# A decoder layer on one core: an embedding gate ahead of the gated unit, the state space some steps later, 64-row taps, and a bias table from the host

## The chip, the cores and the metric

The kernel runs on one core of one Trainium2 chip. The metric is the device time of one execution in microseconds (us), the median of several runs. The engines are called as in the profile: PE is TensorE (matmuls), PEld its weight loads, DVE is VectorE, ACT is ScalarE, POOL is GpSimd, SP is SyncE, whose queue issues nearly all DMAs.

## What is computed

One layer of a hybrid decoder for 256 tokens of width 1024, all in float32. The input x is projected to eight parts; attention (8 heads of 64, one causal block with a bias by distance) and a state space (S5, 32 groups of 16 channels with 64 complex states each) run on some of them, gates on the others, and a normalisation ends it.

```python
proj = x @ w_in[i]
q, k, v, z_a, u, z_s, g_a, g_s = jnp.split(proj, IN_SPLITS, axis=-1)
o_a = moba_attention(heads(q), heads(k), heads(v), rel_bias)
y_a = (o_a * jax.nn.silu(z_a)) @ w_attn_proj[i]
y_s = s5_ssm(u, ssm_a_re[i], ssm_a_im[i], ssm_log_dt[i], ssm_b_re[i], ...)
glu_a, glu_b = jnp.split(jax.nn.gelu(y_s, approximate=False) @ w_glu[i], 2, axis=-1)
y_s = glu_a * jax.nn.sigmoid(glu_b)
y_s = (y_s * jax.nn.silu(z_s)) @ w_ssm_proj[i]
mix = (jax.nn.sigmoid(g_a) * y_a + jax.nn.sigmoid(g_s) * y_s) @ w_out[i]
ple = jax.nn.sigmoid(x @ w_ple_gate[i]) * (p[i] @ w_ple_proj[i])
x = layer_norm(DEEPNORM_ALPHA * x + mix + ple, ln_g[i], ln_b[i])
```

The "embedding gate" is sigmoid(x @ w_ple_gate), computed in two halves of 512 columns, tg0 and tg1. The "gated unit" (glu) needs the state space's output y; the embedding gate needs only x.

## The kernel before, in words

**Units and steps.** All weights are read once, in 62 units of 2 x 128 rows by 512 columns (512 KB). A unit is loaded by SP into one of 5 `raw` buffers, rounded by ACT into `whi` (3 buffers, L144), and the remainder is taken by DVE as `wlo` (3 buffers, L145). PE then multiplies in three terms (xh with whi, xl with whi, xh with wlo). One unit is one step of the main chain: 24 matmuls of 128 x 256 (`t_chunk`) or 12 of 128 x 512 (`n_chunk`). All matmuls are recorded at L149, the line of the helper `mm`, so they are told apart by their tiles: `acc` is the main chain, `aux` everything else. The steps in order of before: u 0 to 3, za 4 to 7, zs 8 to 11, q 12 to 15, k 16 to 19, v 20 to 23, ga 24 to 31, gs 32 to 39, ya 40 to 43, glu 44 to 47, tg0 48 to 51, tg1 52 to 55, and then the embedding projection, ys and w_out.

**Order.** PE executes in the order in which the code is written. On the other engines a scheduler orders the instructions, those of loads and splits with priority. `at(step, f)` says behind which step's matmuls the side work `f` is written; the table `AT` holds most of these numbers. A unit's `whi` takes the place of the one three steps earlier, so ACT can write it only when that step's matmuls have been read.

**Buffers of the side work.** Everything that PE makes beside the main chain goes to PSUM tiles `aux`, and there are four of these. Each is free again only when its last reader, mostly ACT or DVE, is through.

**The state space.** `s5_btT(part)` turns the matrices of B with 8 PE transposes, and ACT copies the two results to `BT` (L385). `s5_xm(part, half)` multiplies them with U in two `aux` tiles, 16 matmuls a block. (A matmul of plain float32 operands stands as two records in the profile, so this block is x32 there.) `s5_kbm(half)` makes the taps of the convolution inside a block of L = 4 tokens, 16 narrow matmuls (x32) into the tile `kp`. `s5_kbd` spreads these on DVE to full 128 x 128 block-diagonal weights `Kbd`; `s5_cabd` does that for the weights `CAb` with a POOL memset and ACT copies (L436). At the end `s5_yt(t)` (4 matmuls with `Kbd` for each t of 4, x8) and `s5_y(t)` (32 narrow matmuls with `CAb`, x64) add up one `aux` tile for each t.

**Attention.** `a_scores` puts two heads' scores in two `aux` tiles, DVE adds the bias from the table `tb` and takes the maximum, `a_exp` makes the exponentials on ACT (L587, behind one table load) and scales them (L592), `a_tr` and `a_out` transpose and multiply with v. The bias table is made by a matmul of `rel_bias` with a one-hot matrix in step 8, a copy, a store of 12 KB to DRAM and a load of 1 MB.

Of the kernel before, what the change touches and what calls it, by code (L numbers as in the profile page):

```python
# [18 lines left out]
P = 128  # L19
# [3 lines left out]
H = 8  # L23
# [6 lines left out]
NEG = -1.0e30  # L30
NWARM = 16

AT = dict(bt=24, x=27, sc=23, kb=27, cb=29, tr=31, out=32, y=35)

MAGIC = 12582912.0
LOG2E = 1.4426950408889634
# [6 lines left out]
TWO_PI = float(np.nextafter(np.float32(2 * math.pi), np.float32(0)))  # L43


C_ID, C_MK, C_J, C_OH = 0, P, P + 8, P + 8 + NPH
C_W = C_OH + 257
# [10 lines left out]
def hybrid_layer_kernel(ctx: ExitStack, tc, xT, x, pT, w_in, w_ap, w_sp, w_out, par, bp, cp,  # L58
# [19 lines left out]
    def aux():  # L78
        return PS("aux", 4)
# [9 lines left out]

    cs = T([P, C_W], "cst")  # L90
    ident = cs[:, C_ID:C_ID + P]
    mask = cs[:, C_MK:C_MK + 8]
    jmul = cs[:, C_J:C_J + NPH]
    onehot = cs[0:32, C_OH:C_OH + 257]

    NRAW, NHI, NLO = 5, 3, 3
    units = []
# [50 lines left out]
    def mm(o, a, b, start, stop):  # L148
        return PE.matmul(o, a, b, start=start, stop=stop, skip_group_check=True)  # L149
# [11 lines left out]
        add_units(w_in, D, COL["gs"] + 512 * n, 512)  # L161
    for n in range(2):
        add_units(w_ap, 512, 512 * n, 512)
    for n in range(2):
        add_units(w_glu, 512, 512 * n, 512)
    for n in range(2):
        add_units(w_pg, D, 512 * n, 512)
    for n in range(2):
        add_units(w_pp, 256, 512 * n, 512)
    for n in range(2):  # L170
# [32 lines left out]
    def par_loads():
        nc.sync.dma_start(cs, cst)
        nc.sync.dma_start(br, bp)
        nc.sync.dma_start(cr, cp)
    dk = T([P, 4], "dk")
    rb = T([32, 8], "rb")
    ptr = T([P, 2, S], "Ct")
    ph = T([P, 2, S], "ph", F32R)  # L210
    pl = T([P, 2, S], "pl", F32R)
# [206 lines left out]
                       st5[f"CA{part}"][:, gp, 0:4, :].rearrange("p n c -> p (n c)"),  # L418
                       part == 0, part == 1)

    def s5_kbd():
        p_ = st5["kp"]
        kb = st5["Kbd"] = T([P, 4, 4, P], "Kbd")
        V.tensor_tensor(out=kb.rearrange("p t u (g c) -> p (t u) g c", c=16),
                        in0=bc(p_[:, 0:256].rearrange("p (tu c) -> p tu c", c=16), 2, 8),
                        in1=bc(bc(mask, 1, 16), 3, 16), op=ALU.mult)
        for t in range(4):
            V.scalar_tensor_tensor(kb[:, t, 0, :], ident, dk[:, t:t + 1], kb[:, t, 0, :],
                                   op0=ALU.mult, op1=ALU.add)
# [83 lines left out]
    yh = []  # L513
    yl = []

    def s5_yt(t):
        p_ = st5[f"yp{t}"] = aux()
        kb = st5["Kbd"]
        for tau in range(4):
            n = (4 - tau) * NJ  # L520
            mm(p_[:, tau * NJ:4 * NJ], kb[:, t, tau, :],
               uT[:, t, 0:4 - tau, :].rearrange("p l j -> p (l j)"), tau == 0, False)

    def s5_y(t):
# [7 lines left out]
        if t == 0:  # L532
            st5["y"] = T([P, 4, S], "U")
# [12 lines left out]
    sm_ = T([P, H, 2], "sms")  # L546

    def a_bias():
        p_ = aux()
        nc.sync.dma_start(rb, relb)  # L550
        mm(p_[0:8, 0:257], rb, onehot, True, True)
        r8 = T([8, 384], "pt", bufs=2)
        V.memset(r8[:, 0:127], NEG)
        A.activation(r8[:, 127:384], p_[0:8, 0:257], AF.Copy)
        rs = dr.tile([8, 384], F32, name="scr_r")
        nc.sync.dma_start(rs, r8)
        nc.sync.dma_start(tb, bass.AP(tensor=rs.tensor, offset=rs.offset,
                                        ap=[[1, P], [384, H], [1, 256]]))

    def rev(h, last, n):  # L560
        a = tb[:, h, :]
# [193 lines left out]
    def ev_glu(n):  # L755
        def f(a):
            if n == 0:
                g = late["ga"] = T([P, 2, 512], "uT", nm="gluA")
                for s in range(2):
                    A.activation(g[:, s, :], a[s], AF.Copy, scale=0.25)  # L760
            else:
                g = late["gb"] = T([P, 2, 512], "U", nm="gluB")
                for s in range(2):
                    A.activation(g[:, s, :], a[s], AF.Tanh, scale=0.5)
                    V.scalar_tensor_tensor(g[:, s, :], g[:, s, :], 1.0, late["ga"][:, s, :],
                                           op0=ALU.add, op1=ALU.mult)
                    V.tensor_mul(g[:, s, :], g[:, s, :], zs[:, s, :])
                late["sh"] = T([P, 4, S], "Ct", F32R, nm="sh")
                late["sl"] = T([P, 4, S], "A1", F32R, nm="sl")
                for s in range(2):  # L770
                    h_ = late["sh"][:, 2 * s:2 * s + 2, :].rearrange("p k s -> p (k s)")
                    A.activation(h_, g[:, s, :], AF.Copy)
                    V.tensor_sub(late["sl"][:, 2 * s:2 * s + 2, :].rearrange("p k s -> p (k s)"),
                                 g[:, s, :], h_.bitcast(F32))
        return f
    for n in range(2):
        t_chunk(4, lambda: (yh[0], yl[0]), ev_glu(n))

    n_chunk(8, xop, ev_tanh(new("tg0", "CAb0", (P, 2, 512))))
    n_chunk(8, xop, ev_tanh(new("tg1", "CAb1", (P, 2, 512))))  # L780

    def ev_pp(n):
# [46 lines left out]
    def at(i, *f):  # L829
        order.setdefault(i, []).extend(f)  # L830
# [4 lines left out]
                f()  # L835
        return g

    at(0, par_loads)
    at(0, *[hp_(f) for f in (s5_scalars, s5_angles, s5_phases)])
    at(1, hp_(s5_abar))  # L840
    at(2, lambda: s5_bt(0), lambda: s5_bt(1))
    at(4, s5_bounce)
    at(8, a_bias)
    at(5, lambda: s5_ca(0), lambda: s5_ca(1))
    at(6, small_loads)
    at(AT["bt"], lambda: s5_btT(0))
    at(AT["bt"] + 1, lambda: s5_btT(1))
# [120 lines left out]
def _constants():  # L968
    c = np.zeros((P, C_W), np.float32)
    c[:, C_ID:C_ID + P] = np.eye(P, dtype=np.float32)  # L970
    c[:, C_MK:C_MK + 8] = (np.arange(P)[:, None] // 16 == np.arange(8)[None]).astype(np.float32)
    c[:, C_J:C_J + NPH] = np.concatenate([np.arange(5), L * np.arange(NJ)]).astype(np.float32)
    for d in range(257):
        b = d if d < 16 else min(31, 16 + int(math.log(d / 16) / math.log(8) * 16))
        c[b, C_OH + d] = 1.0
    return c


def _layout(i):
# [17 lines left out]


# [13 lines left out]
```

## Time and profile before

| what | value |
|---|---|
| time, median of 3 runs | 242.12 us (242.01 to 242.9) |
| the profiled execution | 242.09 us, its span 240.3 us |
| mean granted clock of TensorE in it | 0.995 of full speed |
| busy share of PE, DVE, ACT, POOL | 96%, 78%, 58%, 7% |
| data moved | 44.37 MB, mean 185 GB/s |

The span runs from the first to the last event of the core's engines; the time has 1.8 us more. A row of a timeline gives the start in the span, the busy time from the first instruction to the end of the last of the group, the operation, and in brackets the idle time before it and what released it. Groups overlap slightly, because the next matmul or activation begins before the last has drained.

### The profile page before, as it was taken

To read this page: it belongs to the slowest core of one execution; us is meant where nothing else is said; L and a number is where in the kernel's file an instruction comes from. 1 tells how busy PE (TensorE), PEld (TensorE's weight loads), DVE (VectorE), ACT (ScalarE), POOL (GpSimd) and SP (SyncE) were. 2 spreads that over 40 slices of the span, in tenths; PEclk is the share of its full clock that TensorE was granted. 3 is DMA by queue.
4 is the path that set the end of the run, shared out by engine and by line. 5 is a ranking of instruction groups with operands and counts; after the bars stand their busy time and mean duration, and the time that the engine had idled before them with its cause. 6 is when DMAs were issued, how large, how long until landed. Compare 5 with 4: busy or idle time off the path is not lost.

```text
span 240.3 us, 5066 instructions
## 1 busy us (share of the span) xinstructions
PE 230.3 (96%) x2042; PEld 212.6 (88%) x2042; DVE 188.2 (78%) x333; ACT 140.2 (58%) x222; POOL 15.9 (7%) x17
## 2 busy tenths in 40 slices
PE   8899999999999999999999999999999999999970
PEld 6899999999978899998998999999888889988760
DVE  2879999999899986878999744485674479997395
ACT  4847554845588389999734955335565353775021
POOL 4000000000000005000000000072000000000031
PEclk9999999999999999999999999999999999999998
DMA  5999998977634484323743663664555655660013
GB/s 162 331 343 357 354 238 242 353 232 215 196 93 118 147 255 119 110 92 97 232 150 136 207 213 110 197 245 162 189 174 191 199 202 170 186 190 0 3 44 131
DMA packets 26374, 44.37 MB, mean 185 GB/s; under 512 B 4200, under 2 KB 7280, under 8 KB 26352
## 3 DMA queue, kind: packets, MB, share of 16 engines
q1 hardware_dynamic: 26064, 43.75, 57.5%
q8 instruction: 16, 0.26, 0.4%
q10 hardware_dynamic: 288, 0.31, 0.4%
q14 instruction: 6, 0.05, 0.1%
HBM read 42.47 MB, written 1.59 MB: 183 GB/s over the span
## 4 chain that ended last, share of the span: by engine, by line
PE 77%; ACT 10%; DMA 5%; DVE 4%; SPq 2%; issue 1%; ACTq 0%
PE acc L149 68%; PE aux L149 8%; DMA raw<-in_w_in 5%; ACT whi L144 4%; ACT sc L587 2%; ACT sc L592 2%; ACT CAb L436 1%; DVE wlo L145 1%; SPq L191 1%; SPq L189 1%; DVE xb L930 1%; DVE xb L920 1%; DVE st L910 1%; DVE xb L908 1%; PE aux L598 0%
## 5 line engine op out<-in xcount | busy, mean ns | idle before, releaser
L144 ACT ACTIVATE whi<-raw 128x1024 fp32r<-128x1024 f32 (+2 forms) x71 | 70.7, 997 | 59.9 <-PE acc L149 52.9
L145 DVE TENSOR_TENSOR wlo<-raw,whi 128x1024 fp32r<-128x1024 f32 (+2 forms) x71 | 81.9, 1154 | 30.3 <-ACT whi L144 29.9
L149 PE MATMUL acc<-xh,whi 128*128 128x256 f32 x288 | 47.7, 287 | 0.8 <-ACT whi L144 0.8
L149 PE MATMUL acc<-xl,whi 128*128 128x256 f32 x288 | 45.8, 281 | 0.0
L149 PE MATMUL acc<-xh,wlo 128*128 128x256 f32 x288 | 45.6, 280 | 0.0
L149 PEld LDWEIGHTS acc<-xh,whi 128*128 128x128 f32 x288 | 39.3, 190 | 2.3 <-ACT whi L144 1.3
L149 PEld LDWEIGHTS acc<-xl,whi 128*128 128x128 f32 x288 | 39.3, 189 | 0.0
L149 PEld LDWEIGHTS acc<-xh,wlo 128*128 128x128 f32 x288 | 38.9, 188 | 0.3 <-DVE wlo L145 0.3
L149 PE MATMUL acc<-whi,xh 128*128 128x512 f32 x48 | 19.0, 395 | 0.0
L149 PE MATMUL acc<-wlo,xh 128*128 128x512 f32 x48 | 19.0, 395 | 0.0
L149 PE MATMUL acc<-whi,xl 128*128 128x512 f32 x48 | 19.0, 395 | 0.0
L149 PEld LDWEIGHTS acc<-wlo,xh 128*128 128x128 f32 x48 | 9.0, 188 | 2.2
L149 PEld LDWEIGHTS acc<-whi,xh 128*128 128x128 f32 x48 | 9.0, 188 | 2.1
L149 PEld LDWEIGHTS acc<-whi,xl 128*128 128x128 f32 x48 | 9.0, 188 | 2.1
L149 PE MATMUL acc<-whi,BT 128*128 128x512 f32 (+1 forms) x32 | 9.1, 366 | 0.0
L818 POOL TENSOR_SCALAR xb<-xb 128x1024 f32<-128x1024 f32 x2 | 5.5, 2774 | 42.2 <-DMA xb<-in_x 42.2
L916 ACT ACTIVATE rs<-mv,eps 128x1 f32<-128x1 f32 x2 | 0.6, 294 | 12.1 <-DVE mv L915 12.1
L587 ACT ACTIVATE sc<-sc,nmx 128x128 f32<-128x128 f32 (+1 forms) x16 | 7.0, 442 | 0.0
L149 PEld LDWEIGHTS acc<-whi,BT 128*128 128x128 f32 x32 | 5.7, 188 | 1.1
L193 DVE TENSOR_TENSOR xl<-sc,xh 128x256 fp32r<-128x256 f32 x8 | 3.4, 420 | 4.1 <-ACT xh L192 4.1
L908 DVE TENSOR_TENSOR xb<-acc,xb 128x512 f32<-128x512 f32 (+1 forms) x4 | 2.5, 619 | 5.0 <-PE acc L149 5.0
L928 POOL TENSOR_TENSOR xb<-xb,lng 128x512 f32<-128x512 f32 (+1 forms) x2 | 1.7, 839 | 69.8 <-ACT xb L927 69.8
(254 smaller groups left out, 407.8 us busy)
## 6 DMA issues: line engine op xcount, KB each, us to landing
raw<-in_w_in SPq DMA_DIRECT2D x36, 512.0 KB, 4.7
raw<-in_w_pg SPq DMA_DIRECT2D x8, 512.0 KB, 4.6
raw<-in_w_out SPq DMA_DIRECT2D x8, 512.0 KB, 4.5
raw<-in_w_ap SPq DMA_DIRECT2D x4, 512.0 KB, 5.0
raw<-in_w_glu SPq DMA_DIRECT2D x4, 512.0 KB, 3.9
raw<-in_w_sp SPq DMA_DIRECT2D x4, 512.0 KB, 4.1
raw<-in_w_in SPq DMA_DIRECT2D x7, 256.0 KB, 4.3
sc<-in_xT SPq DMA_DIRECT2D x8, 128.0 KB, 4.0
```

Source lines behind the costliest of these rows:

```text
L144: A.activation(h[:, k, c], r[:, k, c], AF.Copy)
L145: V.tensor_sub(l[:, k, c], r[:, k, c], h[:, k, c].bitcast(F32))
L149: return PE.matmul(o, a, b, start=start, stop=stop, skip_group_check=True)
L189: nc.sync.dma_start(xs[:, kk], xT[:, kk])
L191: nc.sync.dma_start(t[:, k, cc], units[c][:, k, cc])
L193: V.tensor_sub(xl[:, kk], xs[:, kk], xh[:, kk].bitcast(F32))
L436: A.activation(o[rw, :, :, 16 * g2:16 * g2 + 16], st5[f"CA{part}"][rw, :, 1:5, :], AF.Copy)
L587: A.activation(sc[:, h, qs[q]], sc[:, h, qs[q]], AF.Exp, bias=nmx[:, h, q:q + 1], accum_out=sm_[:, h, q:q + 1])
L592: A.activation(sc[:, h, qs[q]], sc[:, h, qs[q]], AF.Copy, scale=sm_[:, h, q:q + 1])
L818: G.tensor_scalar(late["xb"][:, s, :], late["xb"][:, s, :], ALPHA, None, op0=ALU.mult)
L908: V.tensor_tensor(out=xb[:, s, sl], in0=(yo2 if c0 else yo[s][n])[:, 0:c1 - c0], in1=xb[:, s, sl], op=ALU.add)
L910: V.bn_stats(out=stat[s][:, c // 256, :], in_=xb[:, s, c:c + 256])
```

## The change

The diff does four things. The first half of the embedding gate, with its four units, goes from behind the glu to ahead of it (tg0 44 to 47, glu 48 to 51). The table `AT` puts the state space's and the attention's later parts 2 or 3 steps further back. The weights of the taps are made another way: `s5_kt` writes them compactly with ACT copies, stores 512 KB to DRAM and loads it back in 8 DMAs into `tt`, and `s5_yt` multiplies in tiles of 64 rows and 32 columns, for two t at once, 64 matmuls (128 records) a call and two calls. The bias table comes from the host as 1 MB and is loaded by one DMA. Some small loads and `s5_abar` are written at another step, and the constants become smaller. In the rows of the kernel after, the line of `mm` is L147, the split is L142 and L143, the exponentials L594, their scaling L599, the copies to `BT` L378, and those of `CAb` L444.

```diff
-AT = dict(bt=24, x=27, sc=23, kb=27, cb=29, tr=31, out=32, y=35)
+AT = dict(bt=27, x=29, sc=23, kb=27, cb=29, tr=33, out=34, y=38)
...
+    add_units(w_pg, D, 0, 512)
     for n in range(2):
         add_units(w_glu, 512, 512 * n, 512)
-    for n in range(2):
-        add_units(w_pg, D, 512 * n, 512)
+    add_units(w_pg, D, 512, 512)
...
-    def s5_kbd():
-        p_ = st5["kp"]
-        kb = st5["Kbd"] = T([P, 4, 4, P], "Kbd")
-        V.tensor_tensor(out=kb.rearrange("p t u (g c) -> p (t u) g c", c=16),
-                        in0=bc(p_[:, 0:256].rearrange("p (tu c) -> p tu c", c=16), 2, 8),
-                        in1=bc(bc(mask, 1, 16), 3, 16), op=ALU.mult)
+    kscr = dr.tile([512, 4, 64], F32, name="scr_k")
+
+    def s5_kt():
+
+        p_ = st5["kp"][:, 0:256].rearrange("p (t u c) -> p t u c", t=4, u=4)
+        kt = T([P, 4, 4, 16, 4], "kT", nm="kt")
+        G.memset(kt, 0.0)
+        for l in range(L):
+            A.activation(kt[:, :, l, :, l:4].rearrange("p t c u -> p t u c"), p_[:, :, 0:4 - l, :],
+                         AF.Copy)
...
+        nc.sync.dma_start(kscr.rearrange("(t q) l d -> q t (l d)", q=P),
+                          kt.rearrange("q t l c u -> q t (l c u)"))
+        tt = st5["tt"] = T([P, 16, 2, 64], "Kbd", nm="tt")
+        G.memset(tt[:, :, 1, :], 0.0)
+        v = kscr.rearrange("(r m c) l d -> r l c m d", r=2, c=16)
+        for r in range(2):
+            for l in range(L):
+                b0 = 64 * r + 16 * (L - 1 - l)
+                nc.gpsimd.dma_start(tt[b0:b0 + 16, :, 0, :], v[r, l])
...
-    def s5_yt(t):
-        p_ = st5[f"yp{t}"] = aux()
-        kb = st5["Kbd"]
-        for tau in range(4):
-            n = (4 - tau) * NJ
-            mm(p_[:, tau * NJ:4 * NJ], kb[:, t, tau, :],
-               uT[:, t, 0:4 - tau, :].rearrange("p l j -> p (l j)"), tau == 0, False)
+    def s5_yt(t0):
+
+        for t in (t0, t0 + 2):
+            st5[f"yp{t}"] = aux()
+        tt = st5["tt"].rearrange("p m z d -> p (m z d)")
+        for l in range(L):
+            for g2 in range(2):
+                for gpt in range(4):
+                    for r in range(2):
+                        t = t0 + 2 * r
+                        gpp = 4 * (t % 2) + gpt
+                        rw = slice(64 * r, 64 * r + 64)
+                        o = 128 * (2 * gpp + g2) - 64 * g2 + l
+                        mm(st5[f"yp{t}"][32 * gpt:32 * gpt + 32, l * NJ:(l + 1) * NJ],
+                           tt[rw, o:o + 125:4], U[rw, gpp, g2, :], l == 0 and g2 == 0, False)
...
     def a_bias():
-        p_ = aux()
-        nc.sync.dma_start(rb, relb)
-        mm(p_[0:8, 0:257], rb, onehot, True, True)
...
-        nc.sync.dma_start(tb, bass.AP(tensor=rs.tensor, offset=rs.offset,
-                                        ap=[[1, P], [384, H], [1, 256]]))
+        nc.sync.dma_start(tb, relb)
...
+    n_chunk(8, xop, ev_tanh(new("tg0", "CAb0", (P, 2, 512))))
     for n in range(2):
         t_chunk(4, lambda: (yh[0], yl[0]), ev_glu(n))
-
-    n_chunk(8, xop, ev_tanh(new("tg0", "CAb0", (P, 2, 512))))
...
-    at(AT["kb"] + 1, lambda: s5_kbm(1), s5_kbd)
+    at(AT["kb"] + 1, lambda: s5_kbm(1), s5_kt)
...
-    for t in range(4):
-        at(AT["y"] + 2 * t, lambda t=t: s5_yt(t))
-        at(AT["y"] + 1 + 2 * t, lambda t=t: s5_y(t))
-    at(44, load_x)
+    for t in range(2):
+        at(AT["y"] + 4 * t, lambda t=t: s5_yt(t))
+        at(AT["y"] + 1 + 4 * t, lambda t=t: s5_y(t))
+        at(AT["y"] + 3 + 4 * t, lambda t=t: s5_y(t + 2))
+    at(47, load_x)
```

**ACT around the copies to BT.** Before, ACT's queue from the split for step 27 to the second head pair's exponentials reads so; the last four digits of a name count the tiles.

```order
69 L144 ACTIVATE whi_1150<-raw_1027 128x1024
70 L385 ACTIVATE BT_177_1111<-aux_1112 128x512
71 L385 ACTIVATE BT_177_1111<-aux_1118 128x512
72 L144 ACTIVATE whi_1217<-raw_1045 128x1024
73 L385 ACTIVATE BT_185_1178<-aux_1179 128x512
74 L385 ACTIVATE BT_185_1178<-aux_1185 128x512
75 L587 ACT_TABLE_LOAD
76 L587 ACTIVATE sc_158,sms_160<-sc_158,nmx_159 128x128
```

In the kernel after, the same queue has the table load first; here are its rows from the split of step 29's unit to the copies of the taps, with stretches left out.

```order
70 L142 ACTIVATE whi_1237<-raw_1069 128x1024
71 L594 ACT_TABLE_LOAD
...
83 L378 ACTIVATE BT_189_1265<-aux_1266 128x512
84 L378 ACTIVATE BT_189_1265<-aux_1272 128x512
85 L444 ACTIVATE CAb_209_1438<-C_97_504 64x64x16 x2
...
100 L142 ACTIVATE whi_1448<-raw_1235 128x1024
101 L594 ACTIVATE sc_158,sms_160<-sc_158,nmx_159 128x128
...
105 L594 ACTIVATE sc_158,sms_160<-sc_158,nmx_159 128x256
106 L378 ACTIVATE BT_199_1340<-aux_1341 128x512
107 L378 ACTIVATE BT_199_1340<-aux_1347 128x512
```

The copies of both parts now stand behind the table load, the second part's behind all 16 exponentials, four `CAb` copies, eight scaling copies and four splits.

**PE at the same place.** Before, the first product with U (tiles 1299 and 1300) stood two steps behind the second part's transposes (tiles 1179 and 1185, row 364). In the kernel after, PE has these rows around steps 28 and 29, numbered.

```order
419 L376 MATMUL aux_200_1341<-cst_2_82,A1_87_420 128x128 x4
420 L376 MATMUL aux_201_1347<-cst_2_82,A1_87_420 128x128 x4
421 L147 MATMUL aux_192_1288<-C0_97_504,Bbd_84_408 32x64 x4
...
425 L147 MATMUL acc_197_1314<-xh_3_84,whi_187_1237 128x256 x2
...
437 L147 MATMUL aux_207_1420<-U_27_155,BT0_189_1265 64x64 x2
438 L147 MATMUL aux_208_1421<-U_27_155,BT0_189_1265 64x64 x2
```

The product with U is now one step behind the second part's transposes. Its second tile, 1421, is given the buffer of tile 1341, which is free when ACT's row 106 has read it.

**POOL around the taps.** POOL's queue in the kernel after, from the memset of the compact taps on:

```order
8 L420 MEMSET kt_1369 128x1024
9 L441 MEMSET CAb_210_1442 128x2048
10 L432 MEMSET tt_1380 128x16x64
11 L441 MEMSET CAb_209_1438 128x2048
12 L476 MEMSET A_214_1492 128x16
13 L477 MEMSET A_215_1493 128x16
14 L437 DMA tt_1380<-scr_k 16x16x64 x8
15 L497 MEMSET B_231_1611 128x16
```

Eight DMAs stand in a queue that issued none before; they wait for the store of the taps to `scr_k`.

## Rows read from the trace of the kernel before

**Rows 1.** The page, part 1: busy time and instructions of PE.

```profile
PE 230.3 (96%) x2042; PEld 212.6 (88%) x2042; DVE 188.2 (78%) x333; ACT 140.2 (58%) x222; POOL 15.9 (7%) x17
```

**Rows 2.** Waits of the weight loads: waited for, us in total, times, longest.

```profile
PEld aux L149 <- ACT BT L385: 1.2, 2, 0.7
...
PEld aux L149 <- ACT pt L602: 0.4, 1, 0.4
```

**Rows 3.** Timeline of PE, steps 24 to 27: start, busy us, operation.

```profile
75.03 0.23 PE L149 MATMUL aux<-ks,qs 128*128 128x128 f32 x1
...
75.95 0.63 PE L149 MATMUL acc<-xh,whi 128*128 128x256 f32 x4
...
78.78 1.03 PE L383 MATMUL aux<-cst,A 128*128 128x128 f32 x8
...
84.17 1.03 PE L383 MATMUL aux<-cst,A 128*128 128x128 f32 x8
```

**Rows 4.** Timeline of PE, steps 28 and 29: blocks kbm and xm.

```profile
98.07 0.65 PE L149 MATMUL aux<-C,Bbd 128*32 128x64 f32 x32
...
101.67 0.69 PE L149 MATMUL aux<-U,BT 64*64 64x64 f32 x32
102.30 0.74 PE L149 MATMUL acc<-xh,whi 128*128 128x256 f32 x4
```

**Rows 5.** Timeline of ACT, 84 to 107 us.

```profile
84.86 1.06 ACT L385 ACTIVATE BT<-aux 128x512 f32<-128x512 f32 x2
85.94 1.28 ACT L587 ACT_TABLE_LOAD   x1
...
89.81 0.63 ACT L216 ACTIVATE ph<-Ct 128x512 fp32r<-128x512 f32 x1 [0.72 <-DMA Ct<-in_pT]
90.35 1.04 ACT L144 ACTIVATE whi<-raw 128x1024 fp32r<-128x1024 f32 x1
...
98.03 1.48 ACT L592 ACTIVATE sc<-sc,sms 128x128 f32<-128x128 f32 x4
...
102.62 4.25 ACT L436 ACTIVATE CAb<-C 64x1024 f32<-64x1024 f32 x4
106.89 1.09 ACT L726 ACTIVATE Bbd<-acc 128x512 f32<-128x512 f32 x2
```

**Rows 6.** The page, part 5: the exponentials.

```profile
L587 ACT ACTIVATE sc<-sc,nmx 128x128 f32<-128x128 f32 (+1 forms) x16 | 7.0, 442 | 0.0
```

**Rows 7.** Timeline of PE, one tap block and one block of y.

```profile
135.46 1.31 PE L149 MATMUL aux<-uT,Kbd 128*128 128x256 f32 x8
136.57 0.70 PE L149 MATMUL acc<-xh,whi 128*128 128x256 f32 x4
...
139.47 1.10 PE L149 MATMUL aux<-BT,CAb 128*32 128x64 f32 x64
```

**Rows 8.** Timeline of PE, the bias matmul.

```profile
31.55 0.63 PE L149 MATMUL acc<-xh,wlo 128*128 128x256 f32 x4
32.11 0.59 PE L149 MATMUL aux<-cst,rb 32*8 32x257 f32 x2
...
33.21 0.63 PE L149 MATMUL acc<-xl,whi 128*128 128x256 f32 x4
```

**Rows 9.** Windows: stretch, its us, busy us of each engine, PEclk, DMA share, GB/s.

```profile
233.00:236.00 3.00, 0.00 (x0) 0.00 (x0) 2.86 (x8) 0.76 (x2) 1.49 (x3) 1.00 0.25 94
...
237.00:240.00 3.00, 0.00 (x0) 0.00 (x0) 0.39 (x1) 0.00 (x0) 0.00 (x0) 0.65 0.48 170
```

**Rows 10.** Timeline of PE, the start.

```profile
0.76 3.57 PE L87 MATMUL aux<-const-bfloat16-1.0 128*128 128x256 bf16 x16 [0.76 <-PEq L1003]
4.10 1.27 PE L149 MATMUL acc<-xh,whi 128*128 128x256 f32 x4
```

**Rows 11.** DMA issues: KB each, median us to landing.

```profile
scr_u<-uT SPq DMA_DIRECT2D x1, 512.0 KB, 5.7
U<-scr_u SPq DMA_DIRECT2D x8, 64.0 KB, 6.6
```

More of the change, by code (lines that the diff above doesn't have):

```diff
@@ L43 @@
 TWO_PI = float(np.nextafter(np.float32(2 * math.pi), np.float32(0)))
-C_ID, C_MK, C_J, C_OH = 0, P, P + 8, P + 8 + NPH
-C_W = C_OH + 257
+C_J, C_M16, C_ID = 0, NPH, NPH + 16
+C_W = C_ID + P
 def bc(ap, axis, n):
@@ L91, in hybrid_layer_kernel @@
     ident = cs[:, C_ID:C_ID + P]
-    mask = cs[:, C_MK:C_MK + 8]
     jmul = cs[:, C_J:C_J + NPH]
-    onehot = cs[0:32, C_OH:C_OH + 257]
     NRAW, NHI, NLO = 5, 3, 3
@@ L201, in hybrid_layer_kernel @@
     cr = T([P, 2, GP, 16], "crw")
[L203 to L206, printed above, removed]
     dk = T([P, 4], "dk")
-    rb = T([32, 8], "rb")
     ptr = T([P, 2, S], "Ct")
@@ L419, in s5_kbm @@
                        part == 0, part == 1)
-    def s5_kbd():
-        p_ = st5["kp"]
-        kb = st5["Kbd"] = T([P, 4, 4, P], "Kbd")
-        V.tensor_tensor(out=kb.rearrange("p t u (g c) -> p (t u) g c", c=16),
-                        in0=bc(p_[:, 0:256].rearrange("p (tu c) -> p tu c", c=16), 2, 8),
-                        in1=bc(bc(mask, 1, 16), 3, 16), op=ALU.mult)
-        for t in range(4):
-            V.scalar_tensor_tensor(kb[:, t, 0, :], ident, dk[:, t:t + 1], kb[:, t, 0, :],
-                                   op0=ALU.mult, op1=ALU.add)
+    kscr = dr.tile([512, 4, 64], F32, name="scr_k")
[6 more added lines that the diff above has]
+                         AF.Copy)
+        m16 = bc(cs[:, C_M16:C_M16 + 16], 1, 4)
+        for t in range(4):
+            d = kt[:, t, 0, :, 0]
+            d = bass.AP(tensor=d.tensor, offset=d.offset, ap=[list(d.ap[0]), [65, 4], list(d.ap[1])])
+            V.scalar_tensor_tensor(d, m16, dk[:, t:t + 1], d, op0=ALU.mult, op1=ALU.add)
+        nc.sync.dma_start(kscr.rearrange("(t q) l d -> q t (l d)", q=P),
[7 more added lines that the diff above has]
+                nc.gpsimd.dma_start(tt[b0:b0 + 16, :, 0, :], v[r, l])
     def s5_cabd(part):
@@ L531, in s5_y @@
                        st5[f"CAb{part}"][:, gp, l, :], st5[hk][:, gp, :], False, l == 3 and part == 1)
-        if t == 0:
-            st5["y"] = T([P, 4, S], "U")
+        if "y" not in st5:
+            st5["y"] = T([P, 4, S], "uT", nm="y")
             yh.append(T([P, 4, S], "sn", F32R))
@@ L548, in a_bias @@
     def a_bias():
-        p_ = aux()
-        nc.sync.dma_start(rb, relb)
-        mm(p_[0:8, 0:257], rb, onehot, True, True)
[L552 to L556, printed above, removed]
-        nc.sync.dma_start(tb, bass.AP(tensor=rs.tensor, offset=rs.offset,
-                                        ap=[[1, P], [384, H], [1, 256]]))
+        nc.sync.dma_start(tb, relb)
     def rev(h, last, n):
@@ L836, in hp_ @@
         return g
-    at(0, par_loads)
+    at(0, lambda: nc.sync.dma_start(cs, cst))
     at(0, *[hp_(f) for f in (s5_scalars, s5_angles, s5_phases)])
-    at(1, hp_(s5_abar))
-    at(2, lambda: s5_bt(0), lambda: s5_bt(1))
+    at(3, lambda: nc.sync.dma_start(br, bp), hp_(s5_abar), lambda: s5_bt(0), lambda: s5_bt(1))
     at(4, s5_bounce)
     at(8, a_bias)
-    at(5, lambda: s5_ca(0), lambda: s5_ca(1))
+    at(5, lambda: nc.sync.dma_start(cr, cp), lambda: s5_ca(0), lambda: s5_ca(1))
     at(6, small_loads)
@@ L970, in _constants, with _bias @@
     c[:, C_ID:C_ID + P] = np.eye(P, dtype=np.float32)
-    c[:, C_MK:C_MK + 8] = (np.arange(P)[:, None] // 16 == np.arange(8)[None]).astype(np.float32)
     c[:, C_J:C_J + NPH] = np.concatenate([np.arange(5), L * np.arange(NJ)]).astype(np.float32)
-    for d in range(257):
-        b = d if d < 16 else min(31, 16 + int(math.log(d / 16) / math.log(8) * 16))
-        c[b, C_OH + d] = 1.0
-    return c
+    c[:, C_M16:C_ID] = (np.arange(P)[:, None] % 16 == np.arange(16)[None]).astype(np.float32)
+    return c
+def _bias(relb):
+    b = [d if d < 16 else min(31, 16 + int(math.log(d / 16) / math.log(8) * 16)) for d in range(257)]
+    r = np.concatenate([np.full((127, 8), NEG, np.float32), relb[b]]).T
+    return np.ascontiguousarray(np.stack([r[:, p:p + 256] for p in range(P)]))
 def _layout(i):
@@ L995, in _layout @@
         w_pg=a(i["w_ple_gate"])[0], w_pp=a(i["w_ple_proj"])[0],
-        lng=a(i["ln_g"]), lnb=a(i["ln_b"]), relb=a(i["rel_bias"]), cst=_constants())
+        lng=a(i["ln_g"]), lnb=a(i["ln_b"]), relb=_bias(a(i["rel_bias"])), cst=_constants())
 def kernel(**inputs):
```

## The prediction, made before the kernel after was run

> **What bounds the kernel now.** I read the page first: PE is busy for 230.3 of the span's 240.3 us [rows 1], so time comes mostly from PE's own work, and what it waits for is small. The waits of the weight loads say where: 1.2 us on ACT's copies to BT, 0.4 us on the copy of the transposed weights of attention [rows 2]. So nearly all of the gain that a change can have is matmul work taken away; a loss can be any size, since it needs only a wait that is not there now. The timelines of PE and of ACT between 75 and 113 us are then the place to look at, because there the change moves steps, and there ACT has the least room: from the table load at 85.94 to the tanh pair at 106.89 it idles for 0.72 us alone [rows 5]. It is behind there and catches up later; PE doesn't notice, since what PE needs of ACT in this stretch, the splits apart, was copied at 84.86, ahead of it all.
>
> **What is taken away.** The bias matmul: from the group at 31.55 to the one at 33.21 are 1.66 us, where two groups of the main chain take 2 x 0.47 (24 matmuls, six groups, in the 2.83 us from 75.95 to 78.78 [rows 3]), so it costs 0.72 us [rows 8]. The load of the 1 MB table is still there but earlier, with two small DMAs fewer, and the scores that need it start at 75.03 [rows 3], 40 us later: nothing. The waits on BT in steps 24 and 25 and on the transposes in step 32, 1.2 + 0.4 = 1.6 us [rows 2], go with the steps that are moved: -1.6, if nothing takes their place.
>
> **The taps.** A block of `s5_yt` before starts at 135.46 and the chain goes on at 136.57, 1.11 us, and with the slower first group behind it about 1.2 us; four are 4.8 us [rows 7]. After, two blocks of 128 records, in tiles of 64 rows by 32 columns. The trace has no such tile. The nearest row is the block of y, full rows by 32 columns, where four column quarters run beside each other: 64 records busy for 1.10 us, 17 ns each [rows 7]. The block xm, 64 x 64, four tiles too, has 32 records from 101.67 to 102.30, 20 ns each [rows 4]. If the 8 tiles run beside each other twice as densely as 4 do, a block of 128 takes as long as the y block, some 1.2 us with its ends; if they don't, 128 x 17 ns, 2.2 us. Two blocks are 2.4 or 4.4 us, the change is -2.4 or -0.4. I take -2.4, since both rows have as many records at once as their tiles fill the array, and these tiles fill it with 8; -0.4 belongs to the range. The Trainium skill (TensorE: Matmul & The Clock Gate, section "Wait — 56ns, not 53.3ns?") says that the start-to-start time of matmuls never falls below about 25 ns. The y block shows 17 ns a record, so the measurement decides against it for narrow tiles. By that figure two blocks would be an estimated 6.4 us and the change of this term +1.6.
>
> On DVE `s5_kbd` goes, on ACT four copies from PSUM come, which are behind all that is counted below. The weights of the taps now go through DRAM: a store like the one of u, 5.7 us, then 8 loads of 64 KB like those of U, 6.6 us to landing [rows 11], on a queue whose cost no row shows. The copies `kt` end at about 110 us (below), so the store has landed near 116; the first pair is multiplied behind step 38, near 144. If the 8 go one behind the other at 3.5 us each, they just make it; at the 6.6 us that overlapped DMAs take, all are there by 123. Nothing, with a rival for it.
>
> **The step that costs: who reads the buffer of tile 1341.** The rows of PE and ACT in the part on the change show it. The transposes of BT move from steps 24 and 25 to 27 and 28, and the product with U from 27 to 29, so between the second transposes and the product there is one step in place of two. Worse, on ACT the copies to BT were ahead of the table load; now the second part's copies stand behind it, behind 16 exponentials, four CAb copies and more. PE's second tile of the product, 1421, needs the buffer that the first of those copies empties. PE waits in order, so the whole main chain stands still behind it.
>
> When does ACT get there? PE runs without the bias matmul and the BT waits: step 24 starts at 75.95 - 0.72 = 75.23; a step is 2.83 and a block of scores 0.92 (75.03 to 75.95 [rows 3]), so steps 25, 26 and 27 start at 78.98, 82.73 and 86.48. The split of unit 29 needs step 26's reads of `whi`, over at about 85.3; that is where ACT's row 70 of the order starts. What ACT has to do from there to the end of row 106 I take from its own trace: from 85.94 to 106.89, without the 0.72 of idle time, it needs 20.2 us for one table load, 16 exponentials (7.0 us, [rows 6]), three splits, `ph`, four CAb copies (4.25) and 12 scaling copies [rows 5]. The list after has, on top of that, one split (1.0), three copies to BT (1.6, at 1.06 for two) and the tanh pair (1.1), and four scaling copies less (1.4) [rows 5]: 22.5 us. So the buffer is free at 85.3 + 22.5 = 107.8.
>
> When does PE want it? Step 27 ends at 89.31. Its two blocks behind it, transposes (1.03 busy [rows 3], of which the next block overlaps the last 0.1) and kbm (0.65 busy [rows 4], and 0.1 in the slower first group behind it), bring step 28 to 91.0 and its end to 93.85. There the second transposes wait first for the copy of the first part, rows 71 to 83 of ACT's order, which by the same durations (split 1.0, table 1.3, eight exponentials 3.5, two CAb copies 2.1, ph 0.6, split 1.0, BT 0.5) ends at 95.3: with one of their two tiles done meanwhile, 1.0 us lost. Then kbm, step 29 and PE is at the product at 99.5. It waits until 107.8: 8.3 us. Together +9.3.
>
> What is behind it: the splits for steps 30 to 32 are done by then, and ACT needs only the next few entries to be level again, so I see no second stall; the splits for 33 on wait on steps that are later themselves. The same products, four blocks, are made later instead of earlier; moved, not added.
>
> **The swap of tg0 and glu.** It has the same matmuls in another order. The glu's operand y comes 3 steps later and is used 4 steps later; the trace shows no wait before glu now, so nothing is gained. `load_x` is 3 steps later, with the tail some 80 us off: nothing.
>
> **The clock.** After 3 us without a matmul the granted clock is still full (233 to 236) and is 0.65 in the stretch 237 to 240 [rows 9], so it falls between the levels of 2.4 and 1.2 GHz somewhere past 3 us of rest. At the start it works at the lower one: the first four matmuls of the chain take 1.27 us [rows 10] where four take 0.63 busy later [rows 3], and this lasts from 0.76 to about 5.9, some 5 us in which half of the work is done, 2.5 us lost at most. A rest of 8 us should cost about that once more: bounds 0 and 3, taken 2.2.
>
> **The sum**, against the profiled execution's 242.09 us (240.3 and 1.8 around it; the median of the runs is 242.12, the same): -0.7 (bias), -1.6 (old waits), -2.4 (taps), +9.3 (new waits), +2.2 (clock) = +6.8, so 248.9; rounded up a little for the two xm blocks that now stand alone behind a step instead of sharing its end with kbm: 249.2 us.
>
> **The rivals.**
> 1. *The buffer is free in time*, and the kernel is faster. ACT would have to be through with row 106 by 99.5, 8.3 us earlier than its durations say. What speaks for it: an order that the scheduler forms is a list of its own estimates, and ACT hides behind PE everywhere else. Against it: the durations are measured and ACT had no idle time to give in this stretch [rows 5]. It decides at about 6.5 us of stall saved: from there the sum is under zero. Whole: 242.1 - 0.7 - 1.6 - 2.4 = 237.4. Chance 0.05, and 0.05 that part of it makes the sum about nothing (241 to 243.3).
> 2. *The stall is as said and the clock stays full through it*: 249.2 - 2.2 = 247.0. The rest of 8.3 us against [rows 9] speaks against it; that some blocks fall into the wait speaks for it. Chance 0.15.
> 3. *The 64-row tiles don't run 8 at once*, or their weights, picked with a stride of four, load slowly: 249.2 + 2.0 = 251.2, and more if a record takes the 20 ns of xm (2 x 128 x 20 = 5.1, +2.7: 251.9). Chance 0.2.
> 4. *The taps come late through POOL's queue*. It decides at 28 us for the 8 loads. In the Trainium skill (SBUF — State Buffer, on the trap "DVE blocks DMA") a DMA issued from POOL took about 3100 ns beside a DVE copy, 620 alone; by that figure the 8 would take an estimated 25 us, inside the 28. No run here shows one. From rows, at 6.6 us each in a row [rows 11], 53 us, +25; that needs each to wait for the landing of the last, which the 8 loads of U don't do. I give it 0.05, somewhere from 250 to 275.
>
> **How the numbers follow.** My forecast, 249.2 within 248 to 250.5, has 0.5. With rivals 2 and 3 the range is 246.0 to 252.5; what is outside, rival 1, its partial form and most of 4, is 0.15. About 0.5% (1.2 us) is what a measurement of this kernel can tell from no change: faster 0.06, same 0.05, slower 0.89.
>
> **What the profile after would show.** PE's waits have a new first line, `aux` on ACT's copy to BT at L378, about 9 us in two places, the longer about 8; in its timeline step 29's end is near 99.5 and the next step of the chain starts near 108.5 in place of 102.30 [rows 4]. PEclk has a dip around 105 to 113. The chain of waits runs through ACT's exponentials and CAb copies right up to L378. The tap blocks have 128 records in about 1.2 us each. The bias matmul is gone. I am wrong if PE's wait at that place is under 2 us, if PE waits for `tt`, or if the tap blocks take over 2 us.

## The result and the profile after

The kernel after takes 249.57 us (median of 4 runs, 248.40 to 250.64) beside 242.32 before: a ratio of 1.0295, with a 95% interval of 1.0229 to 1.0361. The forecast was 249.2. The profiled execution takes 248.55 us and its span is 246.6, 6.3 more than before.

The page's parts 1 and 2 show that PE is busy for less time than before and idles more: 228.7 us of work in place of 230.3 [rows 1]. In the clock's row two of the 40 slices stand out in the middle, at 0.7 and 0.5.

```profile
PE 228.7 (93%) x2264; PEld 211.0 (86%) x2264; DVE 184.1 (75%) x331; ACT 140.7 (57%) x225; POOL 22.6 (9%) x27
...
PEclk9999999999999999759999999999999999999995
```

The waits of PE name two places, both on ACT's copies to BT, 9.0 us together. The old waits of [rows 2] are gone.

```profile
PE aux L147 <- ACT BT L378: 7.8, 1, 7.8
PE aux L376 <- ACT BT L378: 1.2, 1, 1.2
```

PE's timeline has both. The second transposes stop half way; the product with U stops after its first four records, which go to tile 1420, at the first that goes to 1421.

```profile
92.22 0.60 PE L376 MATMUL aux<-cst,A 128*128 128x128 f32 x4
94.01 0.66 PE L376 MATMUL aux<-cst,A 128*128 128x128 f32 x4 [1.19 <-ACT BT L378]
...
98.10 0.33 PE L147 MATMUL aux<-U,BT 64*64 64x64 f32 x4
106.23 1.12 PE L147 MATMUL aux<-U,BT 64*64 64x64 f32 x28 [7.79 <-ACT BT L378]
107.28 1.22 PE L147 MATMUL acc<-xh,whi 128*128 128x256 f32 x4
...
112.34 0.69 PE L147 MATMUL aux<-U,BT 64*64 64x64 f32 x32
```

ACT's timeline of the same stretch shows what it did meanwhile. It is never idle from 83.72 to 110; the pair of copies that PE waits for comes at 105.59, behind the last exponential.

```profile
83.72 1.06 ACT L142 ACTIVATE whi<-raw 128x1024 fp32r<-128x1024 f32 x1 [2.69 <-PE acc L147]
84.80 1.28 ACT L594 ACT_TABLE_LOAD   x1
...
93.36 1.09 ACT L378 ACTIVATE BT<-aux 128x512 f32<-128x512 f32 x2
94.33 2.12 ACT L444 ACTIVATE CAb<-C 64x1024 f32<-64x1024 f32 x2
...
105.10 0.50 ACT L594 ACTIVATE sc<-sc,nmx 128x256 f32<-128x256 f32 x1
...
105.59 1.06 ACT L378 ACTIVATE BT<-aux 128x512 f32<-128x512 f32 x2
```

From the split's start to the end of the first copy are 83.72 to 106.1, 22.4 us; the prediction had 22.5. Both ends of the wait came earlier than forecast, PE's wish for the buffer at about 98.4 in place of 99.5 and the copy's end at 106.1 in place of 107.8. The windows of the stretch have PEclk as the third value from the end: 0.95 while PE comes to rest, 0.50 while it rests and when it works again, 1.00 from 112 on.

```profile
98.00:102.00 4.00, 0.43 (x6) 0.20 (x4) 1.23 (x1) 4.00 (x11) 0.00 (x0) 0.95 0.00 0
102.00:106.00 4.00, 0.00 (x0) 0.00 (x0) 1.49 (x3) 4.00 (x15) 0.00 (x0) 0.50 0.54 141
...
109.00:111.00 2.00, 2.00 (x11) 2.00 (x11) 0.06 (x1) 1.47 (x5) 0.00 (x0) 0.50 0.46 162
...
112.00:113.00 1.00, 1.00 (x37) 0.80 (x35) 0.00 (x0) 1.00 (x1) 0.64 (x1) 1.00 0.00 0
```

The tap blocks, 128 records each, take 1.57 us (143.78 to 145.35) and 1.64 us, 12 ns a record.

```profile
143.78 1.64 PE L147 MATMUL aux<-U,tt 64*32 64x64 f32 x128
145.35 0.74 PE L147 MATMUL acc<-xh,whi 128*128 128x256 f32 x4
...
159.11 1.72 PE L147 MATMUL aux<-U,tt 64*32 64x64 f32 x128
```

The way through DRAM costs PE nothing here. Both transfers land sooner than those of the kernel before by which the prediction sized them [rows 11]; POOL issues the eight loads from 112.4 to 116.4, each lands within 4.8 us, and PE, which needs `tt` at 143.78, never waits for it.

```profile
scr_k<-kt SPq DMA_DIRECT2D x1, 512.0 KB, 2.9
tt<-scr_k POOLq DMA_DIRECT2D x8, 64.0 KB, 4.7
```

### The profile page after: what moved, and what is told of

Same layout as the page of the kernel before. It is cut to its first block, busy times and chain, and to the rows that moved or that the text cites. A ratio compares the mean times of both kernels' runs of the same rounds, so it can differ in the third digit from the quotient of the medians.

```text
span 246.6 us, 5551 instructions
## 1 busy us (share of the span) xinstructions
PE 228.7 (93%) x2264; PEld 211.0 (86%) x2264; DVE 184.1 (75%) x331; ACT 140.7 (57%) x225; POOL 22.6 (9%) x27
## 4 chain that ended last, share of the span: by engine, by line
PE 79%; ACT 9%; DMA 4%; DVE 3%; SPq 2%; issue 1%; ACTq 0%
PE acc L147 71%; PE aux L147 7%; DMA raw<-in_w_in 4%; ACT sc L594 3%; ACT whi L142 2%; ACT CAb L444 1%; ACT sc L599 1%; SPq L189 1%; SPq L187 1%; DVE xb L936 1%; ACT BT L378 1%; DVE xb L926 1%; DVE st L916 1%; DVE xb L914 1%; PE aux L605 1%
## 5 line engine op out<-in xcount | busy, mean ns | idle before, releaser
L142 ACT ACTIVATE whi<-raw 128x1024 fp32r<-128x1024 f32 (+2 forms) x71 | 70.8, 999 | 69.3 <-PE acc L147 59.1
L143 DVE TENSOR_TENSOR wlo<-raw,whi 128x1024 fp32r<-128x1024 f32 (+2 forms) x71 | 81.2, 1145 | 39.0 <-ACT whi L142 36.5
L147 PE MATMUL acc<-xh,whi 128*128 128x256 f32 x288 | 48.0, 290 | 0.7 <-ACT whi L142 0.7
L147 PE MATMUL acc<-xl,whi 128*128 128x256 f32 x288 | 46.2, 283 | 0.0
L147 PE MATMUL acc<-xh,wlo 128*128 128x256 f32 x288 | 45.5, 280 | 0.1
L147 PEld LDWEIGHTS acc<-xh,whi 128*128 128x128 f32 x288 | 39.7, 193 | 1.9 <-ACT whi L142 1.1
L147 PEld LDWEIGHTS acc<-xl,whi 128*128 128x128 f32 x288 | 39.7, 194 | 0.0
L147 PEld LDWEIGHTS acc<-xh,wlo 128*128 128x128 f32 x288 | 39.1, 191 | 0.3 <-DVE wlo L143 0.3
L147 PE MATMUL acc<-whi,xh 128*128 128x512 f32 x48 | 19.2, 400 | 0.0
L147 PE MATMUL acc<-wlo,xh 128*128 128x512 f32 x48 | 19.1, 398 | 0.0
L147 PE MATMUL acc<-whi,xl 128*128 128x512 f32 x48 | 19.0, 395 | 0.0
L147 PEld LDWEIGHTS acc<-wlo,xh 128*128 128x128 f32 x48 | 9.0, 188 | 2.5 <-DVE wlo L143 0.4
L441 POOL MEMSET CAb<- 128x2048 f32 x2 | 3.6, 1822 | 80.8 <-PE aux L147 80.8
L147 PEld LDWEIGHTS acc<-whi,xh 128*128 128x128 f32 x48 | 9.0, 188 | 2.1
L147 PE MATMUL aux<-U,BT 64*64 64x64 f32 x128 | 3.5, 246 | 7.8 <-ACT BT L378 7.8
L147 PEld LDWEIGHTS acc<-whi,xl 128*128 128x128 f32 x48 | 9.0, 188 | 2.0
L147 PEld LDWEIGHTS aux<-U,BT 64*64 64x64 f32 x128 | 2.8, 152 | 8.5 <-ACT BT L378 7.9
L147 PE MATMUL acc<-whi,BT 128*128 128x512 f32 (+1 forms) x32 | 9.0, 364 | 0.0
L594 ACT ACTIVATE sc<-sc,nmx 128x128 f32<-128x128 f32 (+1 forms) x16 | 7.0, 443 | 0.0
```

The lines of the kernel that those rows point to most:

```text
L142: A.activation(h[:, k, c], r[:, k, c], AF.Copy)
L143: V.tensor_sub(l[:, k, c], r[:, k, c], h[:, k, c].bitcast(F32))
L441: G.memset(o, 0.0)
L594: A.activation(sc[:, h, qs[q]], sc[:, h, qs[q]], AF.Exp, bias=nmx[:, h, q:q + 1], accum_out=sm_[:, h, q:q + 1])
```

## The experiments

All ratios are to the kernel before on the same chip.

**The copies on DVE.** PE's order and the buffers stay; only the engine that copies is another.

```diff
-            A.activation(dst[:, 4 * hf:4 * hf + 4, :].rearrange("p a b -> p (a b)"), p_, AF.Copy)
+            V.tensor_copy(dst[:, 4 * hf:4 * hf + 4, :].rearrange("p a b -> p (a b)"), p_)
```

> The kernel after, with the four copies from PSUM to BT made by DVE instead of ACT; PE's order and the number of buffers stay as they are. Theory (the copy stands behind the exponentials in ACT's queue): both new waits, 1.2 and 7.8 us in the trace of after, go, and with them the stretch at the lower clock (about 2 us), so about 249.6 - 9 - 2 = 238.5 us. Rival (four buffers are too few for this order, whoever copies): PE still waits 3 us or more at the product with U, 243 us or more. Rival (the loss comes from the new taps and loads, not from this place): 247 or more.

Measured: 239.83 us, ratio 0.9892 (0.9855 to 0.9928). DVE copies the second part at 94.80, 11 us earlier than ACT did, and PE goes through the product without a stop:

```profile
93.56 1.03 PE L376 MATMUL aux<-cst,A 128*128 128x128 f32 x8
...
98.14 0.69 PE L147 MATMUL aux<-U,BT 64*64 64x64 f32 x32
```

So four buffers are enough for this product; what was missing is ACT's time. Of the 1.3 us by which it misses the expectation 0.9 stand at the third product (its block takes 1.50 us in place of 0.62), where PE now waits for DVE's reads of the buffer, L485. The rest isn't explained.

```profile
PE aux L147 <- DVE A L485: 0.6, 1, 0.6
```

**The copies on ACT, some entries earlier.** The transposes and copies are written with the scheduler's priority.

```diff
-    at(AT["bt"], lambda: s5_btT(0))
-    at(AT["bt"] + 1, lambda: s5_btT(1))
+    at(AT["bt"], hp_(lambda: s5_btT(0)))
+    at(AT["bt"] + 1, hp_(lambda: s5_btT(1)))
```

> The kernel after, with the transposes of BT and their copies given priority in the scheduler: PE's order and the buffers are the same, and the copies stay on ACT, but the second part's first copy now stands behind the split for step 31 (row 93 of ACT's queue in place of 106), with 10 of 16 exponentials ahead of it. Theory: by the trace of after that split ends at 99.7 and the copy at 100.2, where PE wants the buffer at 98.1, so the wait of 7.8 us becomes about 2.1, the first wait of 1.2 stays, the clock stays full: 5.7 us and some 2 us of clock less, 242 to 242.8 us. Rival (the place in ACT's queue doesn't set the wait): 249 or more.

Measured: 242.77 us, 1.0015 (0.9988 to 1.0042). The waits:

```profile
PE aux L147 <- ACT BT L378: 1.9, 1, 1.9
PE aux L376 <- ACT BT L378: 1.2, 1, 1.2
```

The wait is 1.9 us where 2.1 were expected, and the clock of the profiled execution stays at full speed, at a mean of 0.995; among its other executions are means down to 0.982. So the place in ACT's queue sets the size of the stall.

**The transposes back at step 24.** `AT` with `bt=24`, all else as after.

> The kernel after, with the transposes of BT back behind steps 24 and 25, all else as after. Theory: ACT then copies BT ahead of its table load again, the 9.0 us of new waits go and the old ones of 1.2 us come back, the clock stays full: 249.6 - 9 - 2 + 1.2 = 239.8 us. Rival (the product two steps later, or the new taps, cost the time): 246 or more.

Measured: 241.09 us, 0.9951 (0.9921 to 0.9981). The 9.0 us are gone and the old 0.8 (PE) and 1.2 us (weight loads) are back; it has a wait of 0.4 us on ACT's tanh at 124.69 and one of 0.3 us on DVE's remainder at 35.81 that before hasn't. The rest of the 1.3 us between it and the expectation stays unexplained.

**Work in the place of the wait.**

```diff
             st5["xo"] = [aux(), aux()]
+            if part == 0:
+                for _ in range(NFILL):
+                    PE.matmul(st5["xo"][0][:, 0:256], wz[:, 0:P], wz[:, 0:256], start=True, stop=True)
```

> The kernel after, with 72 matmuls of 256 columns in bf16 on constants put ahead of the first product with U, into the first of its two tiles, which the product then overwrites; at full clock they take 72 x 0.107 = 7.7 us, the length of the wait. They change no result. Theory (a third term of the loss is the clock that falls while PE rests): the wait shrinks to under 1 us, PEclk stays at 1.00, step 30 takes 3.4 us with its block in place of 5.1, and the time is about 2 us less, 247.6. Rival (the clock is worth nothing): 249.6, or more if the matmuls outlast the wait.

Measured: 248.06 us, 1.0246 (1.0206 to 1.0287), 1.5 us less than after by the medians. The intervals of the two ratios overlap, so the totals alone don't show a gain; the traces show where it arises. The timeline shows the 72 matmuls in the wait's place, and step 30 (109.01 to 112.03) in 3.0 us, where after needs 5.06 (107.28 to 112.34):

```profile
100.20 8.25 PE L465 MATMUL aux<-const-bfloat16-1.0 128*128 128x256 bf16 x72
108.38 0.69 PE L148 MATMUL aux<-U,BT 64*64 64x64 f32 x32
109.01 0.74 PE L148 MATMUL acc<-xh,whi 128*128 128x256 f32 x4
...
112.03 0.69 PE L148 MATMUL aux<-U,BT 64*64 64x64 f32 x32
```

From the end of step 29 to the start of the next product the sum is 11.83 us there and 14.24 after (98.10 to 112.34). The product itself goes on 8.2 us behind that end in the one and 8.1 in the other (106.23), so the difference lies behind the wait, where after works at a granted clock of 0.50. The lower clock costs 2.4 us at this place. The rest of the two traces is not the same: ahead of step 28 the run with the filled wait stops for 1.1 us, for DVE, and after doesn't.

**The taps alone, in the kernel before**, at its own steps 35 and 39.

> The kernel before with the new taps alone: compact taps through DRAM and POOL's queue, two blocks of 128 records in place of four of 8, at steps 35 and 39. Theory: blocks of 1.6 us as in the trace of after, so 4.8 - 2 x 1.65 = 1.5 us less, 240.8; ACT's four extra copies (1.3 us) stand ahead of the splits for steps 31 and 32, where PE may lose up to 1 us. Rival (the taps come late through POOL's queue): PE waits for them at step 35, 243 or more. Rival (no matter): 242.3.

Measured: 244.26 us, 1.0085 (1.0053 to 1.0118): slower. The theory misses, and the first rival has the time right by a cause that isn't there: PE doesn't wait for the taps. But ACT's four copies `kt` land in the stretch where ACT is behind, ahead of the transposes of attention and of a split, and PE waits in step 31 for them:

```profile
109.06 0.33 PE L622 MATMUL aux<-cst,sc 128*128 128x128 f32 x1 [0.22 <-ACT kt L430]
...
110.83 0.74 PE L150 MATMUL acc<-xh,whi 128*128 128x256 f32 x4 [1.23 <-ACT whi L145]
...
112.57 0.74 PE L150 MATMUL acc<-xh,wlo 128*128 128x256 f32 x4 [0.53 <-DVE wlo L146]
```

Then the first block of y waits 1.1 us for DVE. So the copies were not free; in the kernel after, where the transposes come at step 33, PE has no wait for them or for the splits behind them.

**The bias table alone, in the kernel before.**

> The kernel before with the bias table from the host alone. Theory: the matmul and its block of 0.72 us in step 8 go, nothing waits for the table: 241.4. Rival (the load of 1 MB, now ahead of unit 9's, delays that unit): PE waits at step 9 by up to the 2.8 us that 1 MB takes at the rate of that stretch, 242 to 244.

Measured: 245.38 us, 1.0125 (1.0096 to 1.0153): slower, and by neither theory. The block in step 8 is gone and the scores start 0.5 us earlier than in [rows 3]. Nothing waits for the load. But with one activation less on ACT and one matmul less on PE the scheduler puts the instructions of ACT and DVE in another order. DVE makes the third and fourth rest of k, `kl` (L704), at 76.19, behind two products for the state space (L403 and L404); before has the third at 72.19, ahead of them. ACT, idle for 0.84 us, waits for that rest, makes k's last two copies from PSUM (L705) at 76.92, behind both of v's, and the scores wait 2.4 us for them. Then the clock dips. In the trace of this run:

```profile
73.82 1.21 DVE L403 TENSOR_TENSOR C<-ncr,Ar 128x1024 f32<-128x1024 f32 x1
...
76.19 1.30 DVE L704 TENSOR_TENSOR kl<-acc,ks 64x512 fp32r<-64x512 f32 x2
...
76.92 1.20 ACT L705 ACTIVATE ks<-acc 64x512 fp32r<-64x512 f32 x2 [0.84 <-DVE kl L704]
```

And in the trace of before, where the order is the other way round:

```profile
72.19 0.70 DVE L714 TENSOR_TENSOR kl<-acc,ks 64x512 fp32r<-64x512 f32 x1
...
77.31 1.23 DVE L404 TENSOR_TENSOR C<-ncr,Ar 128x1024 f32<-128x1024 f32 x1
```

The wait and the clock's row of this run:

```profile
PE aux L149 <- ACT ks L705: 2.4, 1, 2.4
...
PEclk9999999999998899999999999999999999999995
```

**The swap alone, in the kernel before.**

> The kernel before with the first embedding gate ahead of the glu, its units and the load of x moved with it, and nothing else; the state space stays where it was. Theory: the same matmuls in another order, no new wait: 242.2, within 0.6. Rival (the swap itself costs or buys something, by buffers or loads): more than 1 us either way.

Measured: 242.17 us, 1.0004 (0.9989 to 1.0019). The swap by itself costs and buys nothing that shows.

**What sets a tap block's 12 ns a record.** First without the stride, then in another order.

```diff
-                           tt[rw, o:o + 125:4], U[rw, gpp, g2, :], l == 0 and g2 == 0, False)
+                           tt[rw, o // 32 * 32:o // 32 * 32 + 32], U[rw, gpp, g2, :], l == 0 and g2 == 0, False)
```

> The kernel after, with 32 neighbouring columns of the taps' weights in place of every fourth; so y is another one, and only the time counts. In the trace of after a block of 128 records takes 1.57 and 1.64 us, 12 ns a record, between the two cases of the prediction (8.6 and 17 ns). Theory 1 (the stride makes the weight loads dear): the blocks fall to 1.2 us or less. Theory 2 (a tile of 64 rows by 32 columns takes this long to load and start, whatever the stride): 1.5 to 1.7 as before.

```diff
-                for gpt in range(4):
-                    for r in range(2):
+                for r in range(2):
+                    for gpt in range(4):
```

> The kernel after, with the records of a tap block in another order: the four column quarters of one row half behind each other, then those of the other half, where after alternates the halves at each quarter. Theory (a record costs its weight load, 12 ns, in any order): blocks of 1.55 to 1.65 us as before. Rival (neighbours in the same quarter hinder each other): 1.3 us or less; or 2 us, if alternating is what lets the loads overlap.

Measured: a first block of 1.41 us (144.22 to 145.63) without the stride and of 1.56 us (146.19 to 147.75) in the other order.

```profile
144.22 1.48 PE L147 MATMUL aux<-U,tt 64*32 64x64 f32 x128
145.63 0.74 PE L147 MATMUL acc<-xh,whi 128*128 128x256 f32 x4
```

The block without the stride lies between the two theories' 1.2 and 1.5 us, and each of the two times is from one execution: the stride costs about a tenth, and the order nothing. Neither is what sets the 12 ns, and that stays open. The second block without the stride is broken by 0.2 us in which PE waited for nothing that the profile shows, so it tells no more.

**Towards a faster one.** From the copies on DVE three kernels tried to take the last wait away: with the transposes at step 24, with them at 26 and priority for the rotation (`s5_x`), and with the products one step later.

> The kernel after, with the copies to BT on DVE and the transposes back behind steps 24 and 25. With the copies on ACT there, PE waited 1.2 us for them and the time was 241.1. Theory (DVE reaches them sooner than ACT, which has the split first): the 1.2 us shrink to 0.5 or less and the third product finds its buffer free: 240.2 us or less. Rival (DVE is as busy there with the scores' maxima): PE waits as long for DVE, 241 or more.

> The kernel after, with the copies to BT on DVE, the transposes of BT one step earlier (behind steps 26 and 27), and priority for the rotation that reads the first two products with U. In the run with the copies on DVE alone one wait of 0.9 us was left, at the third product, for DVE's reads of the first two, which stood behind a reciprocal that waits for the last exponential; here those reads come some 3 us earlier. Theory: that wait goes, 239.8 - 0.9 = 238.9 us, about 1.3% less than before. Rival (the transposes at step 26 meet the last scores in the four buffers): a new wait of 0.5 to 1.5 us there, 239.8 or more.

> The kernel after, with the copies to BT on DVE and the four products with U one step later (30 to 33 in place of 29 to 32). With the copies on DVE alone, 239.8 us, PE waited 0.9 us at the third product for DVE's reads of the first two. Theory: a step more gives these reads 3 us, and the wait goes: 238.9. Rival (each shift lets the scheduler put ACT's and DVE's instructions in another order, and PE meets another wait): 239.8 or more, with PE's wait on a tile that it does not wait for now.

Measured: 243.50 us, 1.0037 (1.0012 to 1.0061); 244.19 us, 1.0073 (1.0040 to 1.0105); 240.07 us, 0.9924 (0.9898 to 0.9951). The rivals had the time right three times, and the mechanism not always. The largest wait with step 24, and the row of the clock:

```profile
PE aux L147 <- DVE nmx L584: 2.1, 1, 2.1
```

```profile
PEclk9999999999999889999999999999999999999995
```

Here the maxima of the scores, which PE's buffers wait for, start on DVE at 80.46, behind two products for the state space (78.08 to 80.43). The copies to BT come later still, at 82.71, so they are not what PE waits for.

With step 26:

```profile
PE acc L147 <- ACT whi L142: 2.7, 2, 1.8
PE aux L147 <- DVE nmx L584: 1.3, 2, 1.0
```

```profile
PEclk9999999999999999997999999999999999999996
```

The wait at the third product is gone, as the theory has it. The rival's wait at the last scores is there, 1.3 us in two places. The longer one, 1.8 us behind the third product, nobody had forecast: on ACT the split for the next step, at 108.57, stands behind two `CAb` copies (105.71) and two scaling copies. In both runs the granted clock is at 0.50 shortly after the wait, when PE is at work again (82.5 to 85.8 and 111.2 to 114.5), and that costs time beside the waits: with step 24 the six groups from 82.28 on take 4.4 us in place of 2.8.

With the products one step later:

```profile
PE aux L147 <- DVE A L485: 0.6, 1, 0.6
```

The reads by DVE were later too, L485 at 108.48 in place of 105.50, and the wait of 0.6 moved along; it is on the same tile, which is not what the rival said. The version with the copies on DVE and nothing else has the lowest median, 1.1% under before, but the last one's interval overlaps with its own.

## Why the prediction was right

- **The stall** was forecast at 1.0 + 8.3 us and is 1.2 + 7.8; ACT's 22.5 us are 22.4. That its place in ACT's queue is the cause is shown from two sides: another engine copies, and the wait is gone; the copy stands some entries earlier, and it shrinks to what the queue gives. With the transposes back at step 24 it is gone too.
- **The clock** was taken at 2.2 us, and costs 2.4 at that place. That it falls only past 3 us of rest, as the prediction read [rows 9], doesn't hold in the later runs: it was at 0.50 behind waits of 2.4 us (the bias table alone, 77.8 to 81), 2.1 us and 1.8 us (the transposes at steps 24 and 26), and at full speed behind one of 1.9 us (the copies some entries earlier). For the start of before, where the prediction took the lower level from doubled durations, the clock's row has 1.00 from 4.1 to 5.8 us, so the level itself isn't shown there.
- **The bias matmul and the old waits**, -0.7 and -1.6: both are gone in after. That the first is worth less than nothing by itself was not seen: the term was right for the chain and blind to what the scheduler does with the queues of ACT and DVE.
- **The taps** were mis-sized. I took -2.4 us from "8 tiles run beside each other twice as densely as 4", which gave blocks of 1.2 us; they are 1.57 and 1.64. With the slower group behind each, four old blocks cost 4.9 us (1.22 each) and the two new ones 3.6, so the term is -1.3. The other end of the bounds, -0.4, was wrong too: 12 ns a record lies between 8.6 and 17. By the floor of about 25 ns between matmuls (the Trainium skill, TensorE: Matmul & The Clock Gate, section "Wait — 56ns, not 53.3ns?") the blocks would be an estimated 3.2 us; counted by records, these narrow tiles run at half of it, and the measurement decides. Counted by the program's matmuls, of two records each, they take 24.5 and 25.6 ns each, and 22 without the stride.
- **The queue of POOL** and the swap were taken at nothing and are nothing. What I called hidden, ACT's four copies, is so only at the steps of after; the taps alone show the price of another place, a kernel 0.85% slower instead of 0.5% faster.
- **A term was missing.** The profiled execution of after is 2.1 us shorter than the parts of the change make it: the same groups of four matmuls start at another pitch, the time from one start to the next (last section). With it the terms, in the order of the sum, are -0.7 - 1.6 - 1.3 + 10.0 (the two stopped blocks, 2.96 us from 92.22 on and 9.18 from 98.10 on, where the run with the copies on DVE has 1.55 and 0.62) + 2.0 (step 30, 5.06 us in place of 3.02) - 2.1 = 6.3, and the span grew by 6.3. So the forecast came out well in part by luck: two errors of opposite sign, taps dearer by 1.1 and a pitch that it could not know, stand against each other. Without the pitch the terms make 8.4 us and 250.5 us, about where two of the four executions of after lie; the other two lie at 248.5, and the forecast meets the middle, where none is.

## What to carry to other kernels

When a change moves a producer nearer to its consumer, follow the buffer and not only the data: list who empties it, and what stands ahead of that reader in its own queue; the durations of the trace then give the stall to half a microsecond. Where a scheduler orders engines that are as full as ACT and DVE in this stretch, each edit has a second price: it reshuffles their queues, so a part that saves 0.7 us on PE may cost 3, and parts don't add up. In three of the runs here the lower clock followed a wait of some 2 us, so look at the clock's row for each wait. A small job on the full engine (a PSUM copy of half a microsecond) is worth giving to another engine before any step is moved.

## What the hardware showed that was not expected

The same groups of four matmuls of 128 x 256 start 0.47 us after each other in nearly all of the span before, and 0.45 in after from 19 to 61 us and in some later stretches, at the same granted clock of 1.00. Before, ahead of the bias matmul of [rows 8]:

```profile
31.07 0.63 PE L149 MATMUL acc<-xl,whi 128*128 128x256 f32 x4
31.55 0.63 PE L149 MATMUL acc<-xh,wlo 128*128 128x256 f32 x4
```

After:

```profile
31.43 0.62 PE L147 MATMUL acc<-xh,whi 128*128 128x256 f32 x4
31.89 0.62 PE L147 MATMUL acc<-xl,whi 128*128 128x256 f32 x4
```

Of the groups whose next one follows at once, 4 have the shorter pitch before, 119 after, and 14 in the run with the filled wait: 115 x 0.018 = 2.1 us between the first two. It isn't tied to one kernel. Ten such groups stand at the same place, near 150 us in after, in nine of the ten traces of after and of the kernels made from it, and 32 stand from 19 us on in the run with the transposes at step 24 and the copies on ACT; the 92 from 19 to 61 us are in after's trace alone.

The four times of after lie in two pairs, 248.4 and 248.6, 250.6 and 250.6, which are as far apart. The clock doesn't part them, since a mean of 0.969 stands in each pair. The run with the taps' records in another order, in all else the kernel after, has 12 such groups and took 251.04 us, which fits. That the pitch is what parts the pairs is likely but not shown, since each kernel has one trace. What sets it stays open.
